# Hybrid decoder step: spilled S5 gates as whole tiles, log gathers behind the gate sums, S5 output stores on two queues

## The chip, the cores and the metric

The kernel runs on one core of one Trainium2 chip. The metric is the device time of one execution in microseconds. Engines are named as the profile names them: PE (matrix multiply), DVE (vector), ACT (activations), POOL (GpSimd), SP (the queue that issues the weight loads). ACT and POOL issue DMA transfers too, in line with their other work.

## The reference, cut to what matters

One step of a two-layer decoder with 512 prompt tokens and 64 new tokens of 8 running sequences, 576 columns in all. Each layer runs three branches on the same input, gates each branch channel by channel and adds them:

```
gates, u, q, k, v, fg, z, xbc, dt_raw = jnp.split(h @ p['w_in'][l], _in_split_points(), axis=-1)
gates = jax.nn.sigmoid(gates.reshape(bsz, seq, N_BRANCH, D_MODEL) + p['b_gate'][l])
y_s5  = s5_branch(u, ...)            # state-space scan, gelu, gated linear unit
y_fox = fox_prompt(q, k, v, logf)    # or fox_sample(q, k, v, logf, *past): attention with a forget gate
y_ssd = ssd_branch(z, xbc, dt_raw, ...)
merged = (gates[:, :, 0] * (y_s5 @ p['w_branch_s5'][l])
          + gates[:, :, 1] * (y_fox @ p['w_branch_fox'][l])
          + gates[:, :, 2] * (y_ssd @ p['w_branch_ssd'][l]))
out = merged @ p['w_o'][l]
```

For the running sequences the attention reads past keys, values and log forget gates from a paged cache (16 pages of 128 positions per layer, by a page table). Behind the mixer stand a norm, a dense SwiGLU (layer 0) or a two-of-eight expert SwiGLU (layer 1), and a second norm.

## The kernel before, in words

All activations are kept transposed: channels on the 128 partitions, the 576 tokens as columns in two halves of 288 (`HS`). A projection (`dense`, `colblocks`) takes 128 output channels at a time: SP loads the block of weights, ACT and DVE split it into a high and a low part (`wsplit`, L98 and L107), and PE runs three matmuls per 128 input channels and half (`mm3`, L291 to L293). A block with 8 input tiles is 48 matmuls, one with 4 is 24. Results land in PSUM, in two buffers named "mm".

SP's instructions stand in program order, so weights come in the order of the code. The order of the other engines is planned when the kernel is built: the planner simulates the run and gives each engine, as it comes free, the ready instruction that stands first in the program. An instruction that needs a buffer is ready when the ring of that buffer has one free. `tc.issue_after(x)` puts the instructions of a block behind `x` on `x`'s engine. On the chip each engine then works through its list strictly in order.

`mixer(l)` runs: conv and the Mamba branch (`ssd`), keys, queries, values and prompt attention (`kqv_fox`), the S5 scan (`s5_scan_and_out`), attention of the running sequences (`fox_sample`), the spilled gates (`fillers`), the S5 gated unit (`s5_glu`), and the S5 merge (`merge5`). `mixer_end` then loads the attention output (`load_yf`, tile "yft"), gates the Mamba output and merges the other two branches (`merge`).

The places that the change touches:

- **Forget sums and logs.** `kqv_fox` sums the prompt's log forget gates and stores them to CTD (L815, POOL); the prompt attention reads them back per head (cb, L832). `fox_sample` starts with sixteen indirect loads of cached log gates (lfp, L906, POOL), one page each; they depend on nothing but the page table and on the single buffer of lfp. Past keys (kpg, L936) and values (vpg, L962) are gathered on POOL too.
- **S5 output.** The scan's results yg sit with 8 time steps by 16 channels on the partitions; 16 stores per layer (L600, ACT) write them to YD, and two loads (L604, POOL) read them back by channel for the gated unit.
- **Spilled gates.** The gate of the S5 branch is computed early, as filling work for PE: `fillers` calls `gate` for 8 blocks and stores both halves to GD (L1264, ACT). `merge5` calls `gated`, which loads them (L1275, POOL), multiplies them with the projection out of PSUM (L110, DVE, "gt<-gt,mm") and stores the product to MD (L1287, ACT). The half tiles come from ring "h288", four buffers, which the gated unit (g5) and `fill_z` (zt_) use as well. `merge` loads MD back (m5, L1292).
- **Ring "xp"**, four buffers of up to 603 columns: u, conv, keys, queries and values before, yft and m5 after the S5 merge.

Of the kernel before, what the change touches and what calls it, by code (L numbers as in the profile page):

```python
# [8 lines left out]
F32 = mybir.dt.float32  # L9
# [10 lines left out]
P = 128  # L20
# [3 lines left out]
T = NP_ + NB * NS  # L24
HF = T // 2
# [21 lines left out]
def decoder_step(ctx, tc, A, O):  # L47
    nc = tc.nc
    act, dve, pool, pe, sp = nc.scalar, nc.vector, nc.gpsimd, nc.tensor, nc.sync
    consts = ctx.enter_context(tc.tile_pool(name="consts", bufs=1))  # L50
    wk = ctx.enter_context(tc.tile_pool(name="wk", bufs=2))
# [9 lines left out]
    def U(tag, shape, dt=F32, name="u"):  # L61
        return cur["pool"].tile(shape, dt, name=name, tag=tag, bufs=cur["bufs"][tag])
# [160 lines left out]
    for l in range(2):  # L223
        t = consts.tile([P, 16], I32, name=f"pgi{l}")
# [70 lines left out]
    HS = (slice(0, HF), slice(HF, T))  # L295
# [19 lines left out]
    MD = [dr.tile([8, P, T], F32, name=f"MD{l}") for l in range(2)]  # L315
    GD = [dr.tile([24, P, T], F32, name=f"GD{l}") for l in range(2)]
# [4 lines left out]
    YD = [dr.tile([512, 576], F32, name=f"YD{l}") for l in range(2)]  # L321
    CTD = [dr.tile([8, 512], F32, name=f"CTD{l}") for l in range(2)]
# [151 lines left out]
    def s5_scan_and_out(l):  # L474
# [76 lines left out]
        for i, (pn, sn) in enumerate(((5, 12), (6, 13))):  # L551
# [9 lines left out]
            for a in range(2):  # L561
                pool.dma_start(out=O[sn][l].rearrange("b (a g) n -> a b g n", a=2)[a],
                               in_=so[:, 0, a * 64:(a + 1) * 64])
# [33 lines left out]
                stt(yv, y2v[1], 1.0, yv, OP.add, OP.mult)  # L597
        for a in range(2):
            for s in range(8):
                act.dma_start(out=YD[l].rearrange("(g c) (s k) -> s c g k", c=16, s=8)[s, :, a * 16:(a + 1) * 16],  # L600
                              in_=yg[a][s * 16:(s + 1) * 16])
        y5 = [UA([P, 2, 8, 72], name=f"y5{i}") for i in range(2)]
        for i in range(2):
# [154 lines left out]
    def kqv_fox(l, w_in):  # L758
# [53 lines left out]
            tr(pt[:8, i * P:(i + 1) * P], ct[:, i, :], P)  # L812
        c8 = W5("c8")[:8]
        cp(c8, pt[:8])
        pool.dma_start(out=CTD[l], in_=c8)  # L815

        kqv_, kq_, cb_ = {}, {}, {}

# [78 lines left out]
    def fox_sample(l):  # L897
# [4 lines left out]
        ck = A["cache_k"].rearrange("l n p h d -> (l n p) (h d)")  # L902
        cv = A["cache_v"].rearrange("l n p h d -> (l n p) (h d)")
        off = lambda i: bass.IndirectOffsetOnAxis(ap=pgi[l][:, i:i + 1], axis=0)
        for i in range(16):
            pool.indirect_dma_start(out=lfp[:, i, :], out_offset=None, in_=clf, in_offset=off(i))  # L906
        l4 = lf[:64, 4, 0, :]
        for k in range(4):
            for e in range(2):
# [324 lines left out]
    def wload_fd(w_in):  # L1234
# [2 lines left out]
            sp.dma_start(out=raw[:, :, i * 8:(i + 1) * 8], in_=w_in[:, c:c + 8].rearrange("(k p) c -> p k c", p=P))  # L1237
        return raw

    def gate(l, br_, j, tag=None):  # L1240
        o = dense(A["w_in"][l], br_ * 1024 + j * P, 8, X)
        t = []
        for h in range(2):
            t.append(U(tag, [P, HF], F32, name="gt") if tag else
                     wk.tile([P, HF], F32, name="gt", tag="h288", bufs=4))
            c0 = R_BG + br_ * 8 + j
            act.activation(t[h], o[h], AF.Tanh, scale=0.5, bias=prm[l][:, c0:c0 + 1])
        return t
# [11 lines left out]
    def fillers(l):  # L1260
        for br_ in SPILL[l]:
            for j in range(8):
                for h, t in enumerate(gate(l, br_, j)):
                    act.dma_start(out=GD[l][br_ * 8 + j, :, HS[h]], in_=t)  # L1264
        fill_z(l, 0, 4 - NZ[l])

    def gated(l, br_, j, yv):
        wb = A[("w_branch_s5", "w_branch_fox", "w_branch_ssd")[br_]][l]
        tag = "GT" if br_ else None
        if br_ in SPILL[l]:  # L1270
            t = []
            for h in range(2):
                t.append(U(tag, [P, HF], F32, name="gt") if tag else
                         wk.tile([P, HF], F32, name="gt", tag="h288", bufs=4))
                pool.dma_start(out=t[h], in_=GD[l][br_ * 8 + j, :, HS[h]])  # L1275
        else:
            t = gate(l, br_, j, tag)
        o = dense(wb, j * P, 4, yv)
        for h in range(2):
            stt(t[h], t[h], 1.0, o[h], OP.add, OP.mult)  # L1280
        return t

    def merge5(l, yv):
        for j in range(8):
            t = gated(l, 0, j, yv)
            for h in range(2):
                act.dma_start(out=MD[l][j, :, HS[h]], in_=t[h])  # L1287

    def merge(l, yf, ys, mhl):
        def front(j):  # L1290
# [641 lines left out]
```

## Time and profile before

| | us |
|---|---|
| median of 3 timed runs | 2440.81 (2440.51 to 2442.37) |
| the profiled execution | 2439.51 |
| its span, first to last instruction | 2437.9 |
| PE busy / DVE / ACT / POOL | 2282.9 / 1621.9 / 1144.4 / 596.0 |
| mean granted clock of PE | 0.966 |

A span's busy shares are averages over stages, so the rows further down are read stage by stage. A granted clock of 1.00 is 2.4 GHz and 0.50 is 1.2 GHz; a value between them is a window that had both. DMA issues count as busy on POOL; on ACT they stand as "ACTq".

### The profile page before, as it was taken

The page shows a single profiled execution, that of the slowest core. Times are in us where ns is not written, and L with a number is a line of the kernel's source. Part 1 is how long each engine was busy: PE and PEld are TensorE (multiplying, and loading weights), DVE is VectorE, ACT ScalarE, POOL GpSimd, SP SyncE. Part 2 cuts the span into 40 slices and gives each one's busy share as a digit, 9 for nine tenths or more (in the row PEclk, how much of TensorE's full clock was granted, in tenths as well). Part 3 has the DMA queues.
Part 4 walks back from the last instruction along what each step waited for, and adds up shares of the span by engine and source line. Part 5 has one row for each costly group of instructions (what it writes and reads, how often), then busy time and mean ns, then how long its engine had stood idle before and what let it go on. Part 6 is the DMA issues. An engine that isn't in the chain of part 4 may idle for free. (4 is left out here: it accounts for less than half of the span.)

```text
span 2437.9 us, 46161 instructions
## 1 busy us (share of the span) xinstructions
PE 2282.9 (94%) x17037; PEld 2158.8 (89%) x17038; DVE 1621.9 (67%) x4287; ACT 1144.4 (47%) x2553; POOL 596.0 (24%) x879
## 2 busy tenths in 40 slices
PE   8889998889999999999999999898999699999975
PEld 7889887679998999999899888788999599999974
DVE  7986695446478883334765975555447588888856
ACT  4435434425346323223654443353334477777753
POOL 5874233441020110000214332244003410000022
PEclk9999998889999999999999999999999799999997
DMA  8367558473345433223575575766333799999993
GB/s 203 108 209 202 171 158 203 120 228 94 93 134 133 117 121 105 81 87 94 135 207 166 152 184 156 169 182 204 88 92 113 209 267 255 255 256 253 254 256 86
DMA packets 591997, 402.32 MB, mean 165 GB/s; under 512 B 59254, under 2 KB 556199, under 8 KB 591731
## 3 DMA queue, kind: packets, MB, share of 16 engines
q1 hardware_dynamic: 480088, 240.75, 37.3%
q0 software_dynamic: 29008, 90.07, 13.4%
q10 hardware_dynamic: 82666, 68.46, 9.7%
q8 instruction: 136, 2.23, 0.4%
q14 instruction: 99, 0.80, 0.1%
HBM read 330.74 MB, written 68.57 MB: 164 GB/s over the span
## 5 line engine op out<-in xcount | busy, mean ns | idle before, releaser
L107 DVE TENSOR_TENSOR wl<-wr,wh 128x512 fp32r<-128x512 f32 x894 | 622.7, 707 | 382.4 <-ACT wh L98 359.3
L98 ACT ACTIVATE wh<-wr 128x512 fp32r<-128x512 f32 x894 | 552.6, 625 | 523.6 <-PE mm L292 366.7
L291 PE MATMUL mm<-xh,wh 128*128 128x288 f32 (+1 forms) x2048 | 618.9, 302 | 21.3 <-ACT xp L98 10.3
L292 PE MATMUL mm<-xl,wh 128*128 128x288 f32 (+1 forms) x2048 | 614.8, 300 | 0.0
L293 PE MATMUL mm<-xh,wl 128*128 128x288 f32 (+1 forms) x2048 | 612.1, 299 | 0.0
L291 PEld LDWEIGHTS mm<-xh,wh 128*128 128x128 f32 (+1 forms) x2048 | 387.4, 189 | 34.6 <-ACT xp L98 11.5
L292 PEld LDWEIGHTS mm<-xl,wh 128*128 128x128 f32 (+1 forms) x2048 | 387.5, 189 | 6.7 <-issue 4.4
L293 PEld LDWEIGHTS mm<-xh,wl 128*128 128x128 f32 (+1 forms) x2048 | 387.1, 189 | 3.6 <-issue 1.1
L1674 PE MATMUL mm<-xe,wh 128*128 128x352 f32 x448 | 132.1, 356 | 0.0
L1674 PE MATMUL pf<-xe,wh 128*128 128x352 f32 x448 | 130.5, 355 | 0.0
L1675 PE MATMUL pf<-xe,wl 128*128 128x176 f32 x512 | 117.3, 249 | 0.0
L1675 PE MATMUL mm<-xe,wl 128*128 128x176 f32 x512 | 117.1, 249 | 0.0
L291 PE MATMUL mm<-hq,wh 128*128 128x288 f32 x352 | 104.5, 297 | 0.2 <-DVE rf L104 0.2
L293 PE MATMUL mm<-hq,wl 128*128 128x288 f32 x352 | 104.2, 296 | 0.0
L292 PE MATMUL pf<-xl,wh 128*128 128x288 f32 x352 | 104.1, 296 | 0.0
L291 PE MATMUL pf<-xh,wh 128*128 128x288 f32 x352 | 103.9, 295 | 0.0
L293 PE MATMUL pf<-xh,wl 128*128 128x288 f32 x352 | 103.9, 295 | 0.0
L292 PE MATMUL mm<-hq,wh 128*128 128x288 f32 x352 | 103.7, 295 | 0.0
L1675 PEld LDWEIGHTS mm<-xe,wl 128*128 128x128 f32 x512 | 96.6, 192 | 0.0
L1675 PEld LDWEIGHTS pf<-xe,wl 128*128 128x128 f32 x512 | 96.6, 192 | 0.0
L110 DVE SCALAR_TENSOR_TENSOR gt<-gt,mm 128x288 f32<-128x288 f32 x96 | 43.3, 452 | 67.5 <-PE mm L293 52.9
L1674 PEld LDWEIGHTS mm<-xe,wh 128*128 128x128 f32 x448 | 85.4, 191 | 0.0
(665 smaller groups left out, 5448.2 us busy)
## 6 DMA issues: line engine op xcount, KB each, us to landing
wr<-in_w_in_dram SPq DMA_DIRECT2D x112, 512.0 KB
wr<-in_moe_w_gate_dram SPq DMA_DIRECT2D x64, 512.0 KB
wr<-in_moe_w_up_dram SPq DMA_DIRECT2D x64, 512.0 KB
wr<-in_moe_w_down_dram SPq DMA_DIRECT2D x64, 512.0 KB
wr<-in_w_o_dram SPq DMA_DIRECT2D x32, 512.0 KB
wr<-in_ffn_w_gate_dram SPq DMA_DIRECT2D x25, 512.0 KB
wr<-in_ffn_w_up_dram SPq DMA_DIRECT2D x25, 512.0 KB
wr<-in_ffn_w_down_dram SPq DMA_DIRECT2D x24, 448.0 KB
```

Source lines behind the costliest of these rows:

```text
L98: return act.activation(out, in_, AF.Copy)
L107: e.tensor_tensor(out, a, b, op=OP.subtract)
L110: dve.scalar_tensor_tensor(out, a, s, b, op0=op0, op1=op1)
L291: pe.matmul(o, lhsT=wh_[:, a, :m], rhs=x[0][:, k, s], start=(st and k == 0), stop=False)
L292: pe.matmul(o, lhsT=wh_[:, a, :m], rhs=x[1][:, k, s], start=False, stop=False)
L293: pe.matmul(o, lhsT=wl_[:, a, :m], rhs=x[0][:, k, s], start=False, stop=(sp_ and k == kt - 1))
L1674: pe.matmul(o, lhsT=h_[:, k % 4, :], rhs=xf, start=(k == 0), stop=False)
L1675: pe.matmul(o[:, 0:CAP], lhsT=l_[:, k % 4, :], rhs=x[:, k, 0], start=False, stop=False, skip_group_check=True)
```

## The change

Three edits. The spilled gate becomes one tile of 576 columns from ring "xp", with one transfer where there were two (store to GD, load from GD, store to MD). The sixteen log gathers of a layer are put behind that layer's store of the gate sums. The S5 output stores alternate between ACT's and POOL's queue.

```
-                act.dma_start(out=YD[l].rearrange("(g c) (s k) -> s c g k", c=16, s=8)[s, :, a * 16:(a + 1) * 16],
+                (act, pool)[s % 2].dma_start(out=YD[l].rearrange("(g c) (s k) -> s c g k", c=16, s=8)[s, :, a * 16:(a + 1) * 16],
                               in_=yg[a][s * 16:(s + 1) * 16])
...
-        pool.dma_start(out=CTD[l], in_=c8)
+        S["ctd"] = pool.dma_start(out=CTD[l], in_=c8)
...
-        for i in range(16):
-            pool.indirect_dma_start(out=lfp[:, i, :], out_offset=None, in_=clf, in_offset=off(i))
+        with tc.issue_after(S["ctd"].ins):
+            for i in range(16):
+                pool.indirect_dma_start(out=lfp[:, i, :], out_offset=None, in_=clf, in_offset=off(i))
...
+    def gtile(tag=None):
+        if tag:
+            return [U(tag, [P, HF], F32, name="gt") for h in range(2)]
+        t = wk.tile([P, T], F32, name="gt", tag="xp", bufs=4)
+        return [t[:, HS[h]] for h in range(2)] + [t]
+
     def gate(l, br_, j, tag=None):
         o = dense(A["w_in"][l], br_ * 1024 + j * P, 8, X)
-        t = []
+        t = gtile(tag)
         for h in range(2):
-            t.append(U(tag, [P, HF], F32, name="gt") if tag else
-                     wk.tile([P, HF], F32, name="gt", tag="h288", bufs=4))
             c0 = R_BG + br_ * 8 + j
             act.activation(t[h], o[h], AF.Tanh, scale=0.5, bias=prm[l][:, c0:c0 + 1])
         return t
...
     def fillers(l):
         for br_ in SPILL[l]:
             for j in range(8):
-                for h, t in enumerate(gate(l, br_, j)):
-                    act.dma_start(out=GD[l][br_ * 8 + j, :, HS[h]], in_=t)
+                act.dma_start(out=GD[l][br_ * 8 + j], in_=gate(l, br_, j)[2])
...
         if br_ in SPILL[l]:
-            t = []
-            for h in range(2):
-                t.append(U(tag, [P, HF], F32, name="gt") if tag else
-                         wk.tile([P, HF], F32, name="gt", tag="h288", bufs=4))
-                pool.dma_start(out=t[h], in_=GD[l][br_ * 8 + j, :, HS[h]])
+            t = gtile(tag)
+            pool.dma_start(out=t[2], in_=GD[l][br_ * 8 + j])
...
     def merge5(l, yv):
         for j in range(8):
             t = gated(l, 0, j, yv)
-            for h in range(2):
-                act.dma_start(out=MD[l][j, :, HS[h]], in_=t[h])
+            act.dma_start(out=MD[l][j], in_=t[2])
```

## Rows read from the trace of the kernel before

**Rows 1.** The page, first part: busy time, share of the span and instructions.

```profile
PE 2282.9 (94%) x17037; PEld 2158.8 (89%) x17038; DVE 1621.9 (67%) x4287; ACT 1144.4 (47%) x2553; POOL 596.0 (24%) x879
```

**Rows 2.** Windows, layer 0: stretch, length, PE, PEld, DVE, ACT, POOL, clock, DMA, GB/s.

```profile
490.00:495.00 5.00, 0.56 (x5) 0.32 (x3) 0.69 (x1) 0.63 (x1) 3.78 (x5) 0.78 0.62 166
495.00:500.00 5.00, 3.39 (x13) 1.81 (x14) 0.91 (x2) 1.20 (x2) 3.12 (x6) 0.50 0.67 180
500.00:505.00 5.00, 5.00 (x39) 4.01 (x39) 0.49 (x1) 0.97 (x3) 0.80 (x1) 0.70 0.18 59
...
525.00:530.00 5.00, 1.25 (x5) 1.28 (x6) 1.24 (x3) 0.00 (x0) 1.07 (x2) 0.69 0.89 288
530.00:535.00 5.00, 5.00 (x27) 5.00 (x26) 0.94 (x3) 0.63 (x1) 3.16 (x6) 0.63 0.58 169
535.00:540.00 5.00, 5.00 (x40) 5.00 (x39) 3.39 (x5) 2.48 (x5) 4.93 (x8) 1.00 0.94 276
```

**Rows 3.** Waits of PE, 484 to 540 us: us in total, times, longest.

```profile
PE px L233 <- DMA kpg<-in_cache_k_dram,pgi: 6.0, 2, 5.3
PE mm L291 <- DVE gt L110: 4.6, 1, 4.6
```

**Rows 4.** Timeline of POOL, layer 0: start, us, what [idle before <-releaser].

```profile
469.60 0.96 POOL L906 DMA_INDIRECT lfp<-in_cache_logf_dram,pgi  x1 [0.16 <-issue]
...
492.27 0.95 POOL L936 DMA_INDIRECT kpg<-in_cache_k_dram,pgi  x1 [0.30 <-issue]
```

**Rows 5.** Windows, layer 1, S5 merge.

```profile
1660.00:1665.00 5.00, 1.59 (x12) 1.35 (x11) 0.69 (x1) 0.63 (x1) 2.36 (x5) 0.85 1.01 325
1665.00:1670.00 5.00, 2.94 (x12) 2.97 (x13) 0.83 (x2) 0.00 (x0) 2.24 (x4) 0.50 1.07 276
```

**Rows 6.** Waits of PE, 1650 to 1675 us.

```profile
PE mm L291 <- DVE gt L110: 5.5, 1, 5.5
```

**Rows 7.** Timelines of DVE and POOL, layer 0: the ring of gate tiles.

```profile
528.15 0.86 DVE L110 SCALAR_TENSOR_TENSOR gt<-gt,mm 128x288 f32<-128x288 f32 x2 [2.77 <-DMA gt<-GD]
...
531.84 1.07 POOL L1275 DMA_DIRECT2D gt<-GD  x2 [3.26 <-DMA MD<-gt]
```

**Rows 8.** DMA issues: queue, count, KB each, median us from issue to landing.

```profile
gt<-GD POOLq DMA_DIRECT2D x32, 144.0 KB, 3.3
m<-MD POOLq DMA_DIRECT2D x16, 288.0 KB, 3.2
...
yft<-FD POOLq DMA_DIRECT2D x8, 288.0 KB, 5.4
```

**Rows 9.** Timelines of ACT and PE, layer 0: the S5 output.

```profile
443.24 3.82 ACTq L600 DMA_DIRECT2D YD<-yg  x7
447.18 0.53 ACT L967 ACTIVATE ss<-pa,smy 128x320 f32<-128x320 f32 x1 [4.63 <-issue]
...
447.97 1.11 PE L233 MATMUL px<-ident,kpg 128*128 128x128 f32 x4 [5.72 <-ACT yfs L98]
...
456.71 2.33 ACT L117 ACTIVATE y5h<-y 128x512 fp32r<-128x512 f32 x4 [4.60 <-DMA y<-YD]
```

**Rows 10.** Timeline of POOL, layer 0: the gate sums and first key loads.

```profile
123.60 0.55 POOL L815 DMA_DIRECT2D CTD<-c  x1
...
147.69 1.10 POOL L829 DMA_DIRECT2D kT<-KD  x2
```

**Rows 11.** Windows, layer 0, behind the gate sums.

```profile
120.00:140.00 20.00, 18.99 (x148) 17.66 (x146) 19.50 (x60) 11.29 (x26) 16.18 (x33) 1.00 0.65 186
140.00:160.00 20.00, 12.54 (x95) 11.98 (x94) 19.66 (x45) 6.81 (x14) 18.02 (x36) 0.96 0.75 231
...
220.00:240.00 20.00, 20.00 (x152) 19.20 (x151) 11.85 (x29) 9.70 (x24) 3.64 (x4) 1.00 0.80 204
```

**Rows 12.** Windows, layer 1, behind the gate sums.

```profile
1270.00:1290.00 20.00, 20.00 (x164) 19.23 (x163) 12.61 (x27) 12.12 (x31) 2.88 (x8) 1.00 0.40 127
```

## The prediction

> **What bounds the kernel now.** I read the page's busy line first: PE is busy 2282.9 us of a span of 2437.9, 94% [rows 1]. No other engine comes near, and the matrix work is the same before and after, so a change like this one can only be worth what PE now stands idle, or runs at the lower of its two clock levels (a granted clock of 0.50 is 1.2 GHz, 1.00 is 2.4). Next I cut the span into windows and looked for those in which PE is not busy throughout, then asked the waits view who ended the idle time, and read the timeline of the engine so named. Three places touch the lines of the diff.
>
> Place one is layer 0, 490 to 497 us. PE works 0.56 of 5 us and then 3.39 of 5, so 6.05 us are idle [rows 2]; the waits view puts 6.0 of them on gathers of cached keys (kpg) [rows 3]. The timeline of POOL says why a gather is late: from 469.60 on, POOL works off the sixteen log gathers of layer 1, about 0.95 us each with 0.30 behind it, and the key gather at 492.27 stands among them with no wait of its own but its turn ("issue") [rows 4]. These gathers belong to the next layer; nothing in layer 0 reads them.
>
> Place two is the S5 merge, in both layers. PE waits 4.6 us in layer 0 [rows 3] and 5.5 us in layer 1 [rows 6] for the multiply that empties a PSUM bank with a gate (L110 gt). That multiply in turn waits for a gate half to be loaded, and the load waited for the store that frees its buffer: 2.77 us and 3.26 us in these rows [rows 7]. Four buffers of half a block are two blocks of lead, and a block takes PE 24 matmuls, 3.0 us at 40 in 5 us [rows 2], while load and store each take over 3 us to land.
>
> Place three is the S5 output, layer 0 only. ACT issues seven YD stores back to back, 3.82 us, and the softmax behind them starts after 4.63 us of "issue"; PE waits 5.72 us for ACT's copy behind that, and ACT later waits 4.60 us for what is read back from YD [rows 9].
>
> **The change part by part.** The sum is made on the profiled execution, 2439.51 us (its span and 1.6 us around it); the median of the three timed runs is 2440.81, so I take the saving off that.
>
> *Gathers, what they free.* In place one the 6.05 us of idle PE go, and with them the time at the lower clock that followed the idle: busy time times the missing share, 0.56 x 0.22 + 3.39 x 0.50 + 5.00 x 0.30 = 3.3 us [rows 2]. Together 9.3. What is next late is ACT's copy of the transposed keys, which PE then needs at once and with no slack; I take 1.3 off and count **8.0** (bounds 3 and 9.3: the lower one if the key gather turns out to wait for a buffer instead of its turn). At the start of the run POOL also has sixteen gathers fewer, which I cost at nothing: the waits view of the whole run names POOL behind none of PE's waits there.
>
> *Gathers, what they cost.* Sixteen at 1.25 us are 20 us of POOL, now behind the store of the gate sums (CTD). In layer 1 POOL is busy 2.88 of 20 us in the stretch behind that store [rows 12]: hidden. Before layer 0's gathers are read there is room too (3.64 busy of 20 at 220 to 240), but right behind its CTD store at 123.60 POOL has only 3.8 + 2.0 us idle in 40, and PE is short of work from 140 to 160, 12.54 busy of 20 [rows 10, 11]. Queued behind a gather there are POOL's differences for keys and queries, the chunk loads (xc), and the loads of keys and queries (kT, qT). If all sixteen went there, 20 - 5.8 = 14 us of POOL work would slip. As they come last in program order of what POOL has to do there, I expect them spread over the gaps, each delaying its follower by a us at most, with PE covered by the dense projections from 160 us on: **-1.5** (bounds 0 and -14).
>
> *Gate tiles, what they free.* Layer 0: 4.6 us of waiting and 1.25 x 0.31 + 5.00 x 0.37 = 2.2 us of lower clock, 6.8 [rows 2, 3]. Layer 1: 5.5 and 1.59 x 0.15 + 2.94 x 0.50 = 1.7, 7.2 [rows 5, 6]. Together 14.0. Whole tiles in the four buffers of "xp" are four blocks of lead, 12 us of PE, against about 3.3 (store) + 0.5 (issue) + 3.3 (load) + 1 of multiply, 8 us: the ring no longer binds. A load of 288 KB lands no later than one of 144 (3.2 and 3.3 us [rows 8]), so fusing costs nothing there; the first half's store now waits for the second half, 1.5 us, which the longer lead covers. The Trainium skill (DMA: Bandwidth & Descriptors, section "Anatomy of one DMA") gives a fixed 2.0 us plus bytes over 436 GB/s, by which the estimate would be 2.3 and 2.7 us, a slightly longer block; the rows show no such step, and either way it is far inside the lead. Eight issues fewer each for the spill, the load and the store save ACT and POOL time that nobody waits for: nothing.
>
> *Gate tiles, what they cost.* "xp" is also the ring of yft, the attention output that the next merge loads, and of m5. Now those four loads stand idle buffers away; after the change the first must wait for the store of block 4 and the last for that of block 7. Counted from the end of the S5 merge's matmuls, yft 3 is there after 3.3 + 0.5 + 5.4 = 9.2 us [rows 7, 8] and its split into two halves. PE's cover is one gate block, 48 matmuls, 6.0 us, and the first nine of the projection, 1.1: 7.1. So a new wait of 2 to 4 us per layer; it is nothing if the planner puts the second gate block (6.0 us more) ahead, and up to 7 with the lower clock. I take 3 per layer, **14.0 - 6 = 8.0** (bounds 0 and 14). During the spill itself "xp" is shared with the projections of keys, queries and values, but the spill's weights come behind theirs in SP's fixed order, so the two don't overlap.
>
> *YD on two queues.* ACT's seven stores become three or four: 3.5 x 0.55 = 1.9 us less in front of the softmax. On POOL a store is not to be seen; the nearest rows are a gate load, 0.54, and a gather, 0.95 [rows 4, 7], so four take 2.2 to 3.8 against 3.82 for the seven: the read-back starts 0 to 1.6 us sooner. If the planner sets the second half's stores behind the first half's read-back, which waits for a landing, they start 3.3 us late: -3. At best the whole 5.7 us wait goes. I take **2.0** in layer 0, nearer the issue times than either end, and nothing in layer 1, where no such PE wait shows.
>
> Sum: 8.0 - 1.5 + 8.0 + 2.0 = 16.5 us, **2424.3 us**.
>
> The Trainium skill (SBUF — State Buffer, section "SBUF: two separate sides") speaks against two of the three edits: it says that while DVE runs certain SBUF-to-SBUF instructions, GpSimd can't write the descriptors of its own DMAs, and it names a case of 620 ns that became 3100; by that factor, as an estimate, sixteen gathers beside a busy DVE would be 100 us of POOL. The trace doesn't bear it out for issue: DVE is busy 19.66 of 20 us from 140 to 160, and two key loads issued there by POOL took 1.10 us together [rows 10, 11], as 1.07 for two elsewhere [rows 7].
>
> **The rivals.**
> *The merge's new wait takes all that the ring gives* (yft behind the gate stores): for it speaks that 9.2 us and a split stand against 7.1 of cover; against it, that the planner may reorder. The ring's gain falls from 8 to about 1: 16.5 - 7 = 9.5, 2431 us. Chance 0.20.
> *Another wait takes the place of each* (the key gather waits for its buffer, PE waits for ACT's copies, the order of the engines comes out otherwise and eats the rest): what is left is within 0.2%, about 2439 us. For it speaks that every engine's order is planned anew, in all stages; against it, that the named waits end at POOL's queue and a ring of buffers, not at data. Chance 0.15.
> *Slower: the gathers clog POOL in layer 0 behind the CTD store.* Place: 124 to 160 us, price up to 14 us of slip, and since idle PE fell to the lower clock in place one (9.3 us lost for 6.05 idle, factor 1.5), up to 21 us. Less the 18 of the other terms that is 3 us slower, and 7 with the ring's term at half; I put 5, 2446 us. It decides from 12 us of slip on, that is if some fourteen of the sixteen come before the first key load at 147.69. Against it: the gaps later on, and the low place in program order. Chance 0.08. The Trainium skill's rule on descriptors (the page and section named above) would act in the same place, by making each gather longer.
> *All of it* (no new wait, the YD wait gone): 9.3 + 14 + 4 = 27, 2413.5 us. Chance 0.09.
>
> **How the numbers follow.** The forecast, 2424 with 2416 to 2433 as its own range, has 0.48. A difference of 0.2%, 4.9 us, is about what a measurement of this kernel tells from none. Faster by more: 0.48 + 0.20 + 0.09, less a little for the second case's edge, 0.76; within: 0.16; slower: 0.08. The range of 8 in 10 leaves out the slower case, the upper part of "another wait" and the tip of "all of it": 2412 to 2440.
>
> **What would show it.** Right: no log gather on POOL before the CTD store of its layer; in layer 0's S5 merge no wait of PE on kpg and none on the multiply with gt, at a granted clock of 1.00 throughout; gate loads of which four are under way before the first multiply; ACT's run of YD stores no longer than 2 us. Wrong: a wait of PE on the split of yft right behind the S5 merge (then the ring's term was too high); PE busy less than 11 of 20 us between 120 and 180 with gathers in POOL's line (then the gathers' cost was); the same key gather late for another releaser (then place one's term).

## The result, and the profile after

The changed kernel is slower, not faster: 2458.56 us (median of 18 runs, 2445.77 to 2469.06) against 2440.35 us for the kernel before on the same chip (18 runs, 2435.86 to 2447.66). The ratio on record is 1.0066, with a 95% interval of 1.0053 to 1.0080 (the two medians alone give 1.0075). I had forecast 2424.3.

The profiled execution of the changed kernel took 2447.68 us, its span is 2446.0, so it is one of the shorter ones, 11 us below the median. It can show some 8 us of the loss of 18; the other 10 no trace on this chip shows. The first part of the page, as in [rows 1]: PE's work is the same, and its span is 8 us longer.

```profile
PE 2284.4 (93%) x17037; PEld 2159.4 (88%) x17038; DVE 1611.8 (66%) x4287; ACT 1142.1 (47%) x2553; POOL 598.5 (24%) x879
```

The timeline of POOL (start, us, what, idle before and what ended it) shows the first edit at work, against [rows 4] and [rows 10]. Behind each store of the gate sums come sixteen log gathers, nearly without a break: 124.20 to 149.2 in layer 0, 1254.44 to 1278.7 in layer 1. The lines from 364.09 to 535.71 belong to the second edit and are read further down.

```profile
123.35 0.55 POOL L815 DMA_DIRECT2D CTD<-c  x1
124.20 1.07 POOL L907 DMA_INDIRECT lfp<-in_cache_logf_dram,pgi  x1 [0.30 <-issue]
125.57 1.54 POOL L907 DMA_INDIRECT lfp<-in_cache_logf_dram,pgi  x1 [0.30 <-issue]
...
148.20 0.95 POOL L907 DMA_INDIRECT lfp<-in_cache_logf_dram,pgi  x1 [0.30 <-issue]
...
155.41 1.24 POOL L829 DMA_DIRECT2D kT<-KD  x2
...
364.09 1.61 POOL L1276 DMA_DIRECT2D gt<-GD  x3
...
504.77 0.58 POOL L1276 DMA_DIRECT2D gt<-GD  x1 [18.33 <-DMA MD<-gt]
...
524.89 0.54 POOL L1309 DMA_DIRECT2D yft<-FD  x1 [2.98 <-DMA MD<-gt]
...
531.55 3.68 POOL L104 TENSOR_TENSOR xsum<-xh,xl 128x288 f32<-128x288 f32 x3
535.17 0.55 POOL L1309 DMA_DIRECT2D yft<-FD  x1
535.71 1.60 POOL L1292 DMA_DIRECT2D m<-MD  x3
...
1253.58 0.56 POOL L815 DMA_DIRECT2D CTD<-c  x1
1254.44 1.40 POOL L907 DMA_INDIRECT lfp<-in_cache_logf_dram,pgi  x1 [0.30 <-issue]
...
1277.72 0.99 POOL L907 DMA_INDIRECT lfp<-in_cache_logf_dram,pgi  x1 [0.17 <-issue]
...
1322.47 0.54 POOL L830 DMA_DIRECT2D qT<-QD  x1 [2.95 <-DMA QD<-kq]
```

The windows view (columns as in [rows 2]) answers [rows 2] and the second line of [rows 11]. Place one is mended: from 490 to 500 PE is busy 9.90 of 10 us at 2.4 GHz, where it had 6.05 us idle. Behind the S5 merge, 530 to 545, there is a new hole, 7.26 us idle.

```profile
140.00:160.00 20.00, 13.81 (x81) 12.80 (x80) 6.32 (x17) 5.86 (x12) 18.34 (x27) 0.83 0.75 242
...
490.00:495.00 5.00, 5.00 (x39) 5.00 (x39) 3.79 (x7) 3.81 (x10) 0.00 (x0) 1.00 0.30 79
495.00:500.00 5.00, 4.90 (x37) 4.67 (x36) 3.56 (x7) 2.80 (x6) 0.00 (x0) 1.00 0.44 134
...
530.00:535.00 5.00, 3.20 (x16) 2.99 (x17) 3.46 (x4) 2.50 (x5) 4.53 (x5) 0.83 0.96 356
535.00:540.00 5.00, 0.72 (x4) 0.37 (x2) 3.57 (x8) 1.33 (x3) 2.89 (x6) 0.50 0.96 285
540.00:545.00 5.00, 3.82 (x13) 3.18 (x14) 2.94 (x5) 1.65 (x3) 2.68 (x4) 0.50 0.48 171
```

PE's waits (us in total, times, longest) in the stretches of [rows 9], [rows 3], [rows 6] and behind layer 1's gate sums. The waits for kpg (6.0) and for the gate multiply (4.6 and 5.5) have gone from these stretches, but for 0.3 us in layer 1. In their place stand waits for the halves of yft: 5.4 us in layer 0, 2.9 and 2.0 in layer 1. Elsewhere PE still waits for kpg: 7.8 us over the whole run, as against 7.0 before, 4.5 of them at 384 us, where the gather stood in POOL's line behind a gate load. The last line is the load of queries (qT). POOL's timeline has it at 1322.47, issued as the store of the queries landed, with POOL idle for 2.95 us before it: it was late for its data and not for its turn. In the whole of layer 1's mixer PE waits 6.0 us for qT, and not at all in the kernel before.

```profile
PE mm L291 <- ACT y5h L117: 3.4, 2, 3.0
PE pa L950 <- ACT kk L98: 3.0, 2, 2.6
...
PE mm L291 <- ACT yfh L98: 5.4, 1, 5.4
PE mm L291 <- ACT gt L1252: 3.7, 2, 1.9
...
PE mm L292 <- DVE yfl L107: 2.9, 2, 2.6
PE mm L291 <- ACT yfh L98: 2.0, 1, 2.0
...
PE pf L838 <- DMA qT<-QD: 2.8, 1, 2.8
```

For where the time went by stages, I lay the traces side by side at equal work: the columns of all matmuls that PE has started, which are the same sum in all kernels. The planner orders the work differently inside a stage, so I read only at points between stages, here at 116, 600, 1190, 1850 and 2000 us of the kernel before. Each number is what the stage took more (or less) than in the profiled execution of the kernel before, in us.

| kernel | start | layer 0 mixer | dense SwiGLU | layer 1 mixer | router | experts | all |
|---|---|---|---|---|---|---|---|
| the change, profiled execution | -0.3 | -1.0 | 0.5 | 5.2 | 2.4 | 1.4 | 8.2 |
| e1, the change again, another chip | -2.1 | 6.6 | 0.7 | 11.6 | 10.3 | 3.0 | 30.0 |
| e2, gathers only | 0.0 | -8.8 | -0.4 | 10.0 | 7.6 | -1.0 | 7.4 |
| e3, tiles only | 3.9 | 12.0 | 0.5 | 1.2 | 2.9 | -0.6 | 19.9 |
| e4, stores only | 6.5 | 2.9 | 0.1 | -1.2 | 7.9 | 0.0 | 16.3 |
| e5, burst in the SwiGLU | 5.0 | -2.1 | 12.9 | 5.0 | 11.0 | -2.2 | 29.7 |
| e16, the same, plain loads | -2.1 | -0.9 | -0.5 | -0.3 | 7.1 | -4.5 | -1.2 |
| e6, before without gathers | 0.5 | -12.6 | 0.7 | 0.4 | 9.8 | -2.5 | -3.6 |
| e9, gathers spread | 1.0 | 0.4 | 0.4 | 10.1 | 8.4 | -1.2 | 19.0 |
| e13, spread better, two queues | -0.4 | -2.2 | -0.7 | 3.3 | 4.1 | -4.6 | -0.5 |

The chips differ: on the four others that ran the experiments the kernel before itself took 2459.7 to 2464.5 us, and the router's stage is 4 to 11 us longer in most kernels there, whatever they change. No trace of the kernel before was taken there. So times are compared as ratios to the kernel before on the same chip, and of the table only the stages that a kernel touches are read. The ratios are those on record; they lie up to 0.23% from the ratio of the two medians, so I read nothing from a single difference under 0.2%.

### The profile page after: what moved, and what is told of

It reads as the page before. It is cut to its first block, busy times and chain, and to the rows that moved or that the text cites. A ratio compares the mean times of both kernels' runs of the same rounds, so it can differ in the third digit from the quotient of the medians.

```text
span 2446.0 us, 46046 instructions
## 1 busy us (share of the span) xinstructions
PE 2284.4 (93%) x17037; PEld 2159.4 (88%) x17038; DVE 1611.8 (66%) x4287; ACT 1142.1 (47%) x2553; POOL 598.5 (24%) x879
## 5 line engine op out<-in xcount | busy, mean ns | idle before, releaser
L1674 PEld LDWEIGHTS pf<-xe,wh 128*128 128x128 f32 x448 | 85.2, 190 | 0.1
```

The source lines that it names most:

```text
L1674: pe.matmul(o, lhsT=h_[:, k % 4, :], rhs=xf, start=(k == 0), stop=False)
```

## The experiments

**One execution more, and each edit alone.** The first four ran on one chip, where the kernel before took 2464.53 us.

> The changed kernel once more, unchanged, for the trace of another execution: its runs lie between 2446 and 2469 us, those of the kernel before within 2436 and 2448. Theory A (the costs sit in places: gathers behind the gate sums, yft behind the gate stores): a longer execution shows the same waits of PE as the first, some of them longer, 3 to 10 us more idle time and low clock within 120 to 260, 1240 to 1420 or the two merges. Theory B (the planned order of all engines came out worse, and it is tight in other places): the extra time shows in stages that no line of the change touches, the router or the experts among them. Median expected by both: 2452 to 2460.

Measured: 1.0028 of before (1.0004 to 1.0051), median 2465.73 us, above what both theories expected, on a slower chip; profiled execution 2469.56 us. Its waits of PE are those of the first trace, and there are others that the first has none of: PE idle with nothing that the profile shows to wait for, "issue", 6.4 us in all. Two windows of e1 in the middle of layer 0's gathers: ACT does nothing for 5 us, PE falls to 1.38 of 5 us, and the clock goes to half. Of PE's 5.28 us of idle time here 1.6 are issue waits and most of the rest one wait for ACT, which itself stood still for 8.6 us without a releaser that the profile can name.

```profile
135.00:140.00 5.00, 3.34 (x20) 2.48 (x18) 2.35 (x9) 0.00 (x0) 4.09 (x4) 1.00 0.41 105
140.00:145.00 5.00, 1.38 (x5) 1.03 (x6) 1.31 (x3) 1.97 (x5) 4.52 (x10) 0.52 0.39 132
```

Theory A said the excess over the first trace would lie in the mixers; two thirds do, the rest in the router. Neither theory had issue waits.

> The kernel before with the log gathers behind the gate sums alone. Theory A: PE's 6.0 us on kpg with its low clock go (-9.3), sixteen gathers stand behind CTD in both layers and cost 3.4 us between 120 and 260 and 5.2 between 1240 and 1500: 2439 us, 2436 to 2443. My prediction had -6.5: 2434. Theory B: the time is not told by these places; stages that the edit does not touch move by 2 us or more each, and the total can come out anywhere within 2430 to 2460.

```
+        with tc.issue_after(S["ctd"].ins):
+            for i in range(16):
+                pool.indirect_dma_start(out=lfp[:, i, :], ...)
```

Measured: 0.9983 (0.9962 to 1.0004). The table has both sides of the edit: place one's gain in layer 0 (-8.8), and a loss of 10.0 in layer 1's mixer, where I had costed nothing. Of the 10.0 us, 8.2 are lost by 1290, that is beside the gathers (in e1 6.0 of 11.6, in the change's first trace 2.4 of 5.2). PE's timeline towards the end of layer 1's gathers (1245.6 to 1269) shows how: single matmuls that wait for nothing that the profile shows stand apart by 0.4 to 1.0 us.

```profile
1261.00 0.30 PE L293 MATMUL mm<-xh,wl 128*128 128x288 f32 x1 [0.66 <-issue]
...
1262.45 0.38 PE L292 MATMUL mm<-xl,wh 128*128 128x288 f32 x1 [1.01 <-issue]
1263.87 0.29 PE L293 MATMUL mm<-xh,wl 128*128 128x288 f32 x1 [1.04 <-issue]
```

The windows from 1260 to 1280, e2 first, then the kernel before: PE was busy 16.31 of 20 us at a mean clock of 0.83, and before 20.00 at 1.00.

```profile
1260.00:1280.00 20.00, 16.31 (x102) 14.33 (x101) 10.43 (x23) 8.32 (x22) 8.77 (x15) 0.83 0.44 129
```

```profile
1260.00:1280.00 20.00, 20.00 (x161) 19.37 (x159) 13.75 (x32) 10.61 (x26) 3.09 (x8) 1.00 0.60 180
```

> The kernel before with the gate as one tile and one transfer alone. Theory A: no wait of PE on the gate multiply (-14), but waits on yft's halves right behind the S5 merge, 5.4 and 4.6 us with about 4 and 3 of low clock: +3 us net, 2437 to 2446; the merge's rival of my prediction said 2439. My prediction had -8: 2432. Theory B: as for the gathers, other stages move, anywhere within 2430 to 2460.

```
+        t = wk.tile([P, T], F32, name="gt", tag="xp", bufs=4)
...
+            pool.dma_start(out=t[2], in_=GD[l][br_ * 8 + j])
```

Measured: 1.0027 (1.0009 to 1.0046), so no gain; but the trace has 11.2 us of issue waits between 340 and 640 us, beside the gathers that this kernel still has in place one, so the merge can't be read from it.

> The kernel before with the S5 output stores on two queues alone. Theory A: PE's 5.7 us at the softmax behind ACT's seven stores shrink, 2436 to 2440 us (my prediction had -2). Theory B: other stages move, anywhere within 2430 to 2460.

Measured: 0.9998 (0.9978 to 1.0018).

The four traces together gave a third theory, C: of 64 us in which PE waited for nothing shown, all but 0.5 us lay beside a run of indirect loads on POOL. The next four (before: 2463.70 us) test it.

**A burst where nobody waits for POOL.**

> The kernel before; layer 1's sixteen log gathers stand behind the last load of the S5 product (m5, block 7) of layer 0, that is in the dense SwiGLU, where PE stands idle in no trace so far; layer 0's stay at the start of the run. Theory A (a gather costs only the turns that it takes from others in POOL's line): nobody waits for POOL there, so PE has no idle time between 650 and 1190, and place one's 9 us are saved in full: 0.4% less than before, 0.996. Theory C (sixteen indirect loads back to back starve the other engines: in the four traces of the last runs 63 of 64 us in which PE waited for nothing that the profile shows lie within such bursts): in the 20 us of the burst PE shows idle time put down to issue, 2 to 10 us with the low clock behind it, in an execution in which other bursts show it too, and the gain is 0 to 9 us, 0.997 to 1.000.

```
+        with tc.issue_after(S["m57"].ins) if l else nullcontext():
             for i in range(16):
                 pool.indirect_dma_start(out=lfp[:, i, :], ...)
```

Measured: 0.9997 (0.9981 to 1.0012), and the dense SwiGLU took 12.9 us longer. In the kernel before PE has no idle time there (first line, of the kernel before); here is the stretch with the burst, which POOL issues from 652.09 to 672.6:

```profile
660.00:680.00 20.00, 20.00 (x153) 20.00 (x152) 9.13 (x19) 7.98 (x15) 0.00 (x0) 1.00 0.29 80
```

```profile
655.00:660.00 5.00, 5.00 (x40) 5.00 (x39) 2.11 (x5) 1.61 (x3) 3.80 (x4) 1.00 0.59 161
660.00:665.00 5.00, 4.35 (x32) 4.16 (x31) 1.01 (x2) 0.04 (x1) 4.07 (x4) 1.00 0.08 7
665.00:670.00 5.00, 0.58 (x4) 0.34 (x3) 0.00 (x0) 0.50 (x1) 3.78 (x5) 0.82 0.05 3
670.00:675.00 5.00, 3.50 (x12) 2.96 (x12) 0.00 (x0) 0.00 (x0) 1.96 (x3) 0.50 0.05 2
675.00:680.00 5.00, 3.30 (x14) 3.30 (x15) 2.12 (x4) 2.19 (x5) 0.00 (x0) 0.50 0.40 115
```

From about the eighth gather on, with POOL alone at work, the others hardly move until the burst is over: from 665 to 675 PE does 4.08 of 10 us, ACT 0.50 and DVE nothing. Its DMA view of 662 to 675 us (queue, kind: packets, MB, share of 16 engines) shows that in 13 us nothing moved but the gathers:

```profile
DMA packets 314, 0.04 MB, mean 3 GB/s; under 512 B 314, under 2 KB 314, under 8 KB 314
## 3 DMA queue, kind: packets, MB, share of 16 engines
q0 software_dynamic: 314, 0.04, 5.3%
```

So no transfer of weights was slow: the DMA engines were busy 5%, and the view's list of issues has none in these 13 us but gathers. Theory A falls as the whole account: the burst costs where nobody waits for POOL.

The start of the run says the same. Four kernels ran on the other chips with layer 0's sixteen gathers still at the start (e3, e4, e5, e8): there the start took 3.9 to 10.2 us more than in the first chip's trace, with one wait of PE of 10.8 to 15.1 us that begins at some 14 us, when POOL issues the seventh or eighth gather. In the other fourteen it took -2.1 to 1.7 us more.

> The kernel before, with one plain load of the first 2048 rows in the place of the sixteen gathers of each layer: the log gates read are not those of the page table, all other work is left as it is. Theory A: place one's 9 us go, 0.996, and the runs spread as those of before. Theory C: the bursts at 5 to 26 and 463 to 496 are gone or half as long, so besides place one up to 10 us of issue waits go, 0.992 to 0.996, and the runs lie closer together than those of before.

```
+        pool.dma_start(out=lfp, in_=clf[0:2048].rearrange("(i p) h -> p i h", p=P))
```

Measured: 0.9892 (0.9866 to 0.9919), 2437.44 us: 26 us less than before, more than theory C gave it. Place one's 9.3 us are some third of that.

> The changed kernel with the same plain load in the place of the gathers, still behind the gate sums. Against the changed kernel, which stood at 1.003 to 1.007 of before, Theory A: the 3.4 and 5.2 us behind the two gate sums go, 0.999 to 1.003 of before. Theory C: 10 to 20 us go, 0.995 to 0.999 of before, and no issue wait of PE at 124 to 150 and 1250 to 1280.

Measured: 0.9974 (0.9957 to 0.9992), inside theory C's range, and no issue wait at 124 to 150 or 1250 to 1280. In the table's terms layer 1's mixer came down to 3.3. But against e6 the other two edits now stand at +0.8%, which neither theory explains.

> The gate as one tile and one transfer alone, with yft moved out of ring xp into a ring of its own of two buffers. If the merge's loss is yft waiting for the gate stores, PE's waits on yft's halves right behind the S5 merge (5.4 us with 4 of low clock in layer 0, 4.6 with 3 in layer 1) go, with the waits on the gate multiply gone too: 14 us less than before and 9 to 17 less than the tiles alone, 0.994 to 0.996 of before. If the yft loads are late for POOL's order instead, the waits stay and the time is that of the tiles alone, 1.000 to 1.003.

```
-            t = wk.tile([P, T], F32, name="yft", tag="xp", bufs=4)
+            t = U("YF", [P, T], F32, name="yft")        # ring of 2
```

Measured: 1.0041 (1.0021 to 1.0060). PE waited 9.7 us for yft's half in layer 0 all the same: with two buffers, the planned order of POOL had the first yft loads behind two m5 loads, which wait for the stores of the products, and the last two behind two more and the three xsum. It does not decide about ring xp.

**Spread instead of in a burst, with and without the other edits** (one chip, before: 2461.93 us).

> The kernel before, with two log gathers of a layer behind each head's load of the gate sums (cb, eight per layer, some 30 us apart): the same 32 gathers, the same bytes, no burst. Theory C (the burst starves the other engines): no issue wait of PE at 5 to 30, 460 to 500 or 1250 to 1280, and most of what the kernel without gathers gained: 0.989 to 0.994 of before. Theory A (each gather costs its 1.25 us turn in POOL's line wherever it stands): place one's 9 us less some 5 us of turns, 0.997 to 0.999. Theory D (sixteen gathers cost what they cost, in a burst or not): 1.000.

```
+            with tc.issue_after(S[f"cb{i // 2}"].ins):
+                pool.indirect_dma_start(out=lfp[:, i, :], ...)
```

> The changed kernel with the gathers spread in the same way: gate tiles and stores as changed, no burst. If the burst was all that the change lost, 0.989 to 0.994 like the kernel with the spread alone. If the tiles lose by themselves what the kernel without gathers showed (0.9974 against 0.9892), 0.997 to 1.000.

> Spread gathers and the gate as one tile and one transfer, stores as before. Against the spread alone: my prediction's term, -8 us, is 0.3% less; the merge's loss (yft behind the gate stores, 8 to 10 us with low clock in layer 0 and 4 to 6 in layer 1, less 14 that the ring gives) is -0.1 to +0.2%; if it is the tiles that lose 20 us, +0.8%.

> Spread gathers and the S5 output stores on two queues, gate tiles as before. Against the spread alone: my prediction's term, -2 us, is 0.1% less; no effect is within 0.2%; if it is the stores that lose 20 us in the kernel with everything, +0.8%.

| gathers spread | gate in halves | whole gate tiles |
|---|---|---|
| stores on ACT | e9: 0.9965 (0.9945 to 0.9985) | e11: 0.9988 (0.9973 to 1.0003) |
| stores on two queues | e12: 0.9946 (0.9928 to 0.9965) | e10: 0.9990 (0.9973 to 1.0007) |

The spread gains 0.35%, between what A and C gave it. In e9's trace the issue waits at 5 to 30, 460 to 500 and 1250 to 1280 are gone, but layer 1's mixer is 10 us longer with no issue wait in it. Theory A's turns in POOL's line could make it so; that isn't shown, and e13 tests it. The whole tiles lose in both rows, by 0.23 and 0.44%, so it was not the burst alone that the change lost; the two queues gain 0.19% in one column and nothing in the other.

**A better place, and the tiles with yft out of their ring** (before: 2459.72 us; e17 and e18: 2462.49 us).

> The stores on two queues; layer 0's log gathers two behind each head's load of the gate sums, layer 1's two behind each m5 load of layer 0 (13 us apart, in the merge and the dense SwiGLU, where POOL has little to do). Against the spread with the stores (0.9946 of before): layer 1's mixer, which lost some 10 us there, loses 0 to 2, so 0.990 to 0.993. If the loss in layer 1 had nothing to do with the gathers, 0.994 to 0.996.

```
+            with tc.issue_after(S[f"m5{i // 2}" if l else f"cb{i // 2}"].ins):
```

Measured: 0.9917 (0.9889 to 0.9946), 2442.58 us: with the gathers out of it, layer 1's mixer came down from 8.9 us too long in e12 to 3.3 (on another chip; the intervals of the two ratios overlap). Eight of the gathers still stand in one run there, 541 to 555, with no issue wait beside them. Of the versions that read the page table's rows this one has the lowest ratio.

> As e13 with the gate as one tile and one transfer, yft in ring xp as in the change. By the last pairs it loses 0.2 to 0.5% against e13: 0.993 to 0.997; PE waits on yft's halves behind the S5 merge of layer 0, 5 to 8 us.

Measured: 0.9973 (0.9950 to 0.9996), 0.56% above e13, a little more than expected, with PE waiting 6.4 us for yft's half in layer 0, as expected.

> As e14, but yft comes as two half tiles out of ring h288, which the gates have left: two blocks of yft can be loaded during the S5 merge. If the wait in ring xp is what the tiles lose, PE's wait on yft in layer 0 falls from 5 to 8 us to 0 to 2 and the time by 8 to 12 us with the low clock: 0.3 to 0.5% below e14, 0 to 0.3% below e13. If the order of the engines is what loses, the time stays within 0.2% of e14.

```
+            for h in range(2):
+                t = wk.tile([P, HF], F32, name="yft", tag="h288", bufs=4)
+                pool.dma_start(out=t, in_=FD[l][j][:, HS[h]])
```

Measured: 0.9964 (0.9943 to 0.9984), level with e14. The trace doesn't decide: six of layer 1's gathers stood in this merge (525.05 to 534.5), and PE's largest wait there, 10.5 us, is put down to issue although a semaphore that it needed came only 2.6 us before its end.

> As e5 (layer 1's sixteen loads in one burst in the dense SwiGLU, layer 0's at the start), but each a plain load of 128 rows of the same 32 bytes, not those of the page table. If any sixteen small loads back to back starve PE, idle time put down to issue of 2 to 10 us at 650 to 690 as in e5 and 0.997 to 1.000 of before. If it takes indirect loads, no idle time there, none at 5 to 30 either, and 0.990 to 0.996.

Measured: 0.9897 (0.9866 to 0.9927). Sixteen plain loads of the same size, closer together than the gathers, leave PE untouched; POOL's line and two windows of PE in the same stretch as in e5:

```profile
645.80 8.47 POOL L907 DMA_DIRECT2D lfp<-in_cache_logf_dram  x16
```

```profile
640.00:660.00 20.00, 20.00 (x153) 20.00 (x152) 8.97 (x17) 6.93 (x14) 9.00 (x17) 1.00 0.40 102
660.00:680.00 20.00, 20.00 (x153) 20.00 (x152) 9.59 (x20) 7.36 (x14) 0.00 (x0) 1.00 0.32 93
```

Against e5, each taken against the kernel before on its own chip, the whole run is 1.0% shorter by the ratios and 0.7% by the medians, some 18 to 25 us for two bursts of sixteen. Sixteen small loads back to back are not enough. Two things differ, though: the loads are indirect in e5, and they keep POOL at work for 20.5 us instead of 8.47; which of the two it takes, this pair doesn't tell.

> As e13 (no whole tiles), with layer 1's log gathers four behind each of the last four m5 loads of layer 0, 13 us apart, clear of the S5 merge. Runs of four cost PE at most 3 us in the traces so far: 0.989 to 0.993 of before, as e13, and the merge of layer 0 without issue waits.

Measured: 0.9945 (0.9924 to 0.9966), above its range and less of a gain than e13, though the intervals overlap. The dense SwiGLU, now with three of the four groups of four gathers, took 0.5 us more than before: four at a time, 19 us apart, cost next to nothing.

> As e17 with the gate as one tile and one transfer and yft as half tiles in ring h288. If yft behind the gate stores is what the tiles lose: PE's waits at the gate multiply (5 to 9 us a layer in e13) are gone, the first two blocks of yft are there in time, and only the last two can be late, by up to 6 us where POOL's line has them behind the m5 loads: 0 to 0.4% below e17. If the tiles lose elsewhere, by the order of all engines, 0.2 to 0.5% above e17 although the merge itself is not longer.

Measured: 0.9953 (0.9933 to 0.9972), 0.08% above e17, inside both intervals. The two differ in the tiles of gate and yft alone, and no log gather stands in their S5 merges. PE's waits in the merges of layer 0 and 1, e17 first, then e18:

```profile
PE mm L291 <- DVE gt L110: 7.0, 7, 1.6
...
PE mm L291 <- DVE gt L110: 5.2, 1, 5.2
PE mm L291 <- ACT gt L1248: 3.0, 2, 1.7
```

```profile
PE mm L291 <- ACT yfh L98: 9.5, 1, 9.5
...
PE mm L291 <- ACT yfh L98: 6.3, 1, 6.3
```

Neither case came as it was put: waits for the gate product are exchanged for a wait for yft, longer than the 6 us that I had allowed, even with yft out of ring xp. Of its eight halves four fit, and the other four were loaded from 538.47 on, behind m5 loads and xsum in POOL's line. The kind of wait matters too: from 12 us before the first product store to 75 behind it, e17's seven short waits cost no time at the lower clock, and e18's single long one 2.9 us.

## Why the prediction was wrong, point by point

**Gathers, what they free: right in its place.** The step had 8.0 us (3 to 9.3). In the change's trace the wait on kpg and the low clock behind it are gone from 490 to 500, and e2's layer 0 is 8.8 us shorter, the gathers that it moved there included. It was their turn in POOL's line, as [rows 4] said. In the change's own trace layer 0 is only 1.0 us shorter: place one's 9.3 and the S5 merge's 6.8 went, and the new hole of 10.1 and the 4.5 us for kpg at 384 came, much as the rival "another wait takes the place of each" had it. The start of the run, which I had put at nothing, is worth 4 to 10 us on the chips where the burst costs there.

**Gathers, what they cost: failed, by a price that the step did not have.** It had -1.5 us, from two statements, both wrong. "I expect them spread over the gaps, each delaying its follower by a us at most": all sixteen went to POOL at once behind the store, and the first key load came at 155.41 instead of 147.69. They were not alone: POOL had been busy 16.18 of 20 us there [rows 11], and the S5 preparation that it did there before came later. Why the planner put the gathers first is not on record. "Hidden" in layer 1, from POOL's 2.88 busy of 20 us: e2 lost 10.0 us in that mixer. The bounds ("0 and -14") were for layer 0 only, and rested on the idea that a gather costs others its turn. The runs show a second price, which no row of mine could bound: in some executions PE, ACT and DVE themselves stop beside a burst of indirect loads. The strongest evidence is e5 against e16, the same program but for the kind of load (and on another chip): 12.9 us against -0.5 in a stage where PE is otherwise busy throughout, and 0.9997 against 0.9897 for the whole. Over the eighteen traces of the experiments PE's issue waits come to 168 us, and 166 of them lie inside runs of three or more indirect loads or within 12 us behind, stretches that make up 8 to 13% of a span. (59 of the 168 stand before instructions that wait for no semaphore at all; in the others a real wait can have a part.) 62 of the 168 lie in layer 1's router, where every kernel has a run of seventeen indirect loads. On the first chip it shows none, which fits the router's 4 to 11 us more on the others.

The kernel before has two such bursts as well, one at the start, where PE waits for its first inputs anyway, and one in place one. The change moved layer 1's to a stretch where PE is busy throughout, and layer 0's to one where it is short of work only from 140 us on. So it may have lost more on the first chip because the kernel before lost little there. On the second chip e3 and e4 show what the kernel before pays for the burst at the start, and the change stands at 1.0028, half the loss or less. For the first chip this is argued and not shown: neither profiled execution there shows an issue wait. Of the 5.2 us that the change's trace lost in layer 1's mixer, 2.4 stand by 1290 and 4.1 between 1320 and 1330, at the wait for qT; the slower executions, 11 us above the profiled one in the median, left no trace.

**Gate tiles, what they free and cost: failed, the rival's case and more.** The sum had 14.0 us freed less 6 for a new wait on yft, so 8.0 saved; alone the tiles came out 0.27% above before (e3), some 7 us lost. The waits for the gate multiply did go, and yft's came. With the wait for a gate ahead of it (ACT gt) and the low clock, the hole from 530 to 545 cost 7.26 + 2.8 = 10.1 us in layer 0, where I had taken 3. Idle time and time lost to the low clock from 12 us before the first product store to 75 (layer 1: 90) us behind it, in us:

| | gate in halves | whole tiles |
|---|---|---|
| layer 0 | 9.9 (e2), 8.1 (e17) | 13.8 (the change), 13.9 (e18) |
| layer 1 | 10.1 (e2), 12.7 (e17) | 10.3 (the change), 11.9 (e18) |

I had expected 3.8 and 4.2 less; layer 0 has 4 to 6 more, layer 1 about the same. The statement that failed is "now those four loads stand idle buffers away". They were not idle: in the kernel before they hold yft, loaded during the merge and split 17 us later. The view of tile yft in layer 0 (line, engine, count: duration ns min/median/max, first and last start), of the kernel before:

```profile
L1309 POOL DMA_DIRECT2D yft<-FD x4: 537/538/539, 519.7 to 521.3; - x4
L98 ACT ACTIVATE yfh<-yft x4: 667/672/675, 538.1 to 539.8; 128x576 fp32r<-128x576 f32 x4
```

and of the change, where the splits come as the loads land, and the last load is 14 us later:

```profile
L1309 POOL DMA_DIRECT2D yft<-FD x4: 537/537/549, 519.1 to 535.2; - x4
L98 ACT ACTIVATE yfh<-yft x4: 668/682/686, 524.1 to 540.4; 128x576 fp32r<-128x576 f32 x4
```

Nor was it ring xp alone that held the last load until 535.17. The product store issued at 521.0 let the third load go at 524.89, 3.9 us later; by the same time (an estimate) the last store, issued at 524.2, had landed by some 528.1. The load then stood behind other loads and three additions of 3.68 us (xsum) in POOL's line. I had counted the ring and forgotten the queue: 9.2 us from the end of the merge's matmuls until yft 3 was there. The last of them starts at 523.35, and the split of yft 3 comes at 540.4, 17 us later.

```profile
523.35 0.29 PE L293 MATMUL mm<-yh,wl 128*128 128x288 f32 x1
```

The lead that the gates won, yft lost. In time the whole tiles lost in all five pairs with the gathers out of the burst: 0.23, 0.44, 0.56, 0.47 and 0.08% (the last inside its interval). In the traces of these pairs the two mixers together took 4 to 9 us longer with whole tiles, 0.2 to 0.35%, the larger part in layer 0. Where the rest of the larger losses lies stays open.

**YD on two queues: too small to tell.** 2.0 us were taken; alone 0.9998, with the spread 0.19% (4.7 us) and nothing. PE's 5.72 us of [rows 9] went in the change's trace, but its waits from 436 to 470 fell only from 10.8 to 9.6 us in all, since new ones came (kk, 3.0). POOL took eight of the sixteen stores there, though ACT's longest run of them was still 3.00 us, where I had named 2.

**The sum.** Of the terms, +8.0 for place one came; -1.5 was -10 in layer 1 alone in e2 (there the change's first trace is 5.2 longer with everything); +8.0 for the tiles was -4 or worse; +2.0 for the stores can't be told from what came. By the single edits on the second chip, gathers, tiles and stores came to -0.17, +0.27 and -0.02%, where the sum had -0.27, -0.33 and -0.08. The gathers came near their forecast there although their cost was far off, on a chip where the kernel before pays for its bursts too: that is luck. The tiles' term is the one furthest off, by some 15 us. That the result would be slower I had given 0.08, with the right suspect (gathers behind the gate sums) in the wrong layer and at a price made of POOL's turns. Of the signs that I named for a right forecast, four gate loads were under way before the first multiply (364.09 and one at 376.19; the fifth waited 18.33 us for the first product's store), PE's two waits in the S5 merge were gone, and ACT's run of stores was too long. Of those for a wrong one, the wait on yft's split behind the merge was there; PE busy under 11 of 20 us from 120 to 180 was not (13.81 from 140 to 160, as against 12.54 in [rows 11]), since the price fell on layer 1. The Trainium skill's rule that certain SBUF-to-SBUF instructions of DVE keep GpSimd from writing descriptors (SBUF — State Buffer, section "SBUF: two separate sides") names a case of 620 ns that became 3100. No such factor shows here: with DVE busy 18.34 of 20 us the gathers at 124 to 140 took 0.95 to 1.54 us each, against 0.95 where DVE is quiet (e5). Whether DVE's instructions there are of the kind that the rule means, no run shows.

## What to carry to other kernels

Don't move a run of indirect loads by where its queue has room; look at what the other engines do meanwhile, and break it up: two to four at a time, some 20 to 30 us apart (e9, e17), where no other load is due. A buffer that is "free" in a ring is often a prefetch of the next stage, so before sharing it, see in the tile's view when it is loaded and when read; and count the queue that reloads it as well as the ring. Where a planner orders the engines, price an edit at the spot where it will put the work as soon as it is ready, not where there is room, and test edits one by one and in pairs, for one that gains can hide one that loses.

## What the runs showed of the hardware

Beside sixteen indirect loads of 128 rows of 32 bytes, issued by POOL some 1.3 us apart, PE, ACT and DVE nearly stood still for some 10 us from about the eighth on, with the DMA engines 5% busy (e5); sixteen plain loads of the same size, issued in 8.47 us, did nothing of the kind (e16), and three groups of four, 19 us apart, cost 0.5 us in the same stage (e17). It happens in some executions and on some chips: the two profiled executions on the first chip show none, each of the eighteen on the others shows some. What it is that is held up is not shown. In e5 no packet of the instruction queues moved between 662 and 675 us. The next one, at 676.1, came after PE's first restart (669.97) and shortly before its second (676.70), so a late load of code is neither proven nor ruled out.
